# Pooling's buffers moved into the upper half of Y, late loads of the heads, and one PSUM bank for a head's two value products

## The chip, the cores and the metric

The kernel runs on one core of a Trainium2 chip. The metric is the device time of one execution in microseconds (us), the median of several runs.

## What is computed

A two-layer decoder trunk on x of 512 positions by 2048 channels, fp32. The change lies in the even layer, whose mixer is:

```
z = h @ w_in                                   # 2048 x 12288
a_in, a_gate, q, k, v, b_gate = split(z)       # a: 1024 wide, q/k/v: 3 groups x 8 heads x 128
ya = causal_pool_mixer(a_in, pool_w, pool_scale) * silu(a_gate)
yb = dilated_attention(q, k, v, cos, sin) * silu(b_gate)
return concatenate([ya, yb]) @ w_out
```

The pooling mixer takes causal means over windows of 2, 4, 8 and 16 positions for four groups of channels, subtracts the input and multiplies by a 256x256 matrix for each group. The attention has 8 heads; each head adds three patterns: group 0 is a window of 128 positions in natural order, groups 1 and 2 take positions of one residue modulo 4 together, so their queries stand in a permuted order (residue r first, then i, for position 4i + r). One softmax denominator serves all three.

## The kernel before

Every fp32 weight is split into a high part (`whi`, ScalarE, line 69) and a rest (`wlo`, VectorE, line 70), and each product is three TensorE matmuls. SyncE loads weights in 512 KB chunks into 4 raw buffers (`wraw`, line 111). A split chunk is a part, and 4 parts can stand ready. The program is a list of stages, one part each (`run_section`). Most of the input projection goes by `pair_item`: two 128-channel units u and v computed with shared half products, in stages s0 to s7. Stage s0 (lines 300 to 304) makes 24 narrow products (256 columns) in a bank and ScalarE copies half of it to u's buffer (line 294); s1 makes 12 more and is copied too; s3 and s3b make 24, s5 and s7 another 24, and s4 and s6 together 24 wide ones (512 columns). Stage s2 of a pair, which ends u, is put behind s1 of the next pair.

The first section is the attention's. Its q and k rows of the three groups of a head take turns in 8 slots, Y[:, 8] to Y[:, 15]; the last head (7) has slots 2 to 7, and slots 0 and 1 hold group 2 of head 6. V of groups 0 and 2 stands in Y[:, 0:8]. A head's attention (lines 665 to 742) is a generator that is advanced a step after each stage, so that a head's softmax runs beside the next head's projection: scores (lines 680 and 692), mask, maximum over keys (line 709, GpSimd), exponentials (lines 716 and 719, ScalarE), sum over keys (line 709 again), the value products (lines 725 to 732), then the reciprocal of the denominator, two multiplications (lines 738 to 740) and a store by GpSimd's queue to DRAM (`ybd`, line 741). The value products of group 0 go to bank `oa`, those of groups 1 and 2 to bank `ob` in permuted order; line 735 copies oa to SBUF, and line 736 adds ob to it with the order undone by a stride of 4.

After the section, lines 1053 to 1055 run out what is left of the last head and release its pool `att`. The pool `mixp`, opened at line 1057, takes the same memory, and the first access to a tile of a new pool waits for the release of the pool that was there, that is, for the store of the last head too. In `mixp` stand the four row buffers `xp` of the pooling (and of its gates), the split results `ph` and `pl` and others. The running sums `pa`, `pb` and `t` stand in Y[:, 4:8]. Lines 1066 and 1067 load the eight stored heads into Y[:, 8:16] on SyncE's queue as slots come free.

The pooling section runs four pairs for the rows (`a_after` makes sums, means and the split), two items of small products (`mix_item`), three pairs and two single items for the gates. `split_y(range(8, 16))` (lines 565 and 566) reads the loaded heads in the middle of the last single item. A scheduler orders each engine's instructions by readiness in a model of the time and by place in the program; `later` pins an instruction behind what was traced before it on its engine. Engines issue in order.

Of the kernel before, what the change touches and what calls it, by code (L numbers as in the profile page):

```python
# [13 lines left out]
F32 = mybir.dt.float32  # L14
FR = mybir.dt.float32r
AF = mybir.ActivationFunctionType
OP = mybir.AluOpType
AX = mybir.AxisListType

P = 128  # L20
D = 2048
S = 512
# [116 lines left out]
def trunk(ctx: ExitStack, tc: tile.TileContext, x, xt, out, ewv, ewz, ewo, epw, epost,  # L139
          owv, owz, owo, opost, osg, osb, oswt, osbias, cblob, rope, pcol):  # L140
    nc = tc.nc
# [27 lines left out]
    def sbank(name):  # L169
        return pss.tile([P, S], F32, tag="s", name=name)  # L170
# [450 lines left out]
    def vtile(g, t):  # L621
        return V1[:, t, :] if g == 1 else Y[:, 2 * g + t, :]
# [6 lines left out]
    def perm_in(ap):  # L629
        return ap.rearrange("p (i r) -> p r i", r=4)  # L630

    def perm_out(ap):
        return ap.rearrange("p (r i) -> p r i", r=4)
# [31 lines left out]
    def attention(h, qk, gates):  # L665
        vc = slice((h % 4) * P, (h % 4) * P + P)
        sa = att.tile([P, 4, 256], F32, tag="sa", name=f"sa{h}")
        sg = att.tile([P, 2, S], F32, tag="sg", name=f"sg{h}")

        def temp(name):  # L670
            return att.tile([P, S], F32, tag="tmp", name=f"{name}{h}", bufs=3)

        own, prev = sa[:, :, 0:P], sa[:, 0:3, P:]
        q, k = qk["q0"], qk["k0"]
        mA = cb[:, C_MA:C_MA + 256]
        b0 = sbank(f"sa{h}").rearrange("p (n k) -> p n k", n=2)
        b1 = sbank(f"sb{h}").rearrange("p (n k) -> p n k", n=2)
        for m in range(4):
            b, w_ = (b0, b1)[m // 2][:, m % 2, :], 256 if m < 3 else P
            nc.tensor.matmul(b[:, 0:w_], k[:, P * m:P * m + P], q[:, P * m:P * m + w_], start=True, stop=True)  # L680
        nc.vector.scalar_tensor_tensor(sa[:, 0:2, :], b0, SCALE, mA[:, None, :].to_broadcast([P, 2, 256]),
                                       op0=OP.mult, op1=OP.min)
        sal = sa.rearrange("p n k -> p (n k)")
        for m in (2, 3):
            w_ = 256 if m < 3 else P
            nc.vector.scalar_tensor_tensor(sa[:, m, 0:w_], b1[:, m - 2, 0:w_], SCALE, mA[:, 0:w_],
                                           op0=OP.mult, op1=OP.min)
        for g in (1, 2):
            b = sbank(f"sg{h}_{g}")
            for r in range(4):  # L690
                t = slice(P * r, P * r + P)
                nc.tensor.matmul(b[:, t], qk[f"k{g}"][:, t], qk[f"q{g}"][:, t], start=True, stop=True)
            mB = cb[:, C_MB + P * (g - 1):C_MB + P * g]
            nc.vector.scalar_tensor_tensor(sg[:, g - 1, :].rearrange("p (r i) -> p r i", r=4),
                                           b.rearrange("p (r i) -> p r i", r=4), SCALE,
                                           mB[:, None, :].to_broadcast([P, 4, P]), op0=OP.mult, op1=OP.min)

        def natural(t):
            return t.rearrange("p (r i) -> p i r", r=4)

        def reduced(op, rop, name):
            u, v = temp(f"{name}u"), temp(f"{name}v")
            nc.vector.tensor_tensor(u, sg[:, 0, :], sg[:, 1, :], op=op)
            nc.vector.tensor_tensor(v.rearrange("p (i r) -> p i r", r=4), natural(u),
                                    sa[:, :, 0:P].rearrange("p n (i r) -> p n i r", r=4), op=op)
            v3 = v[:, P:].rearrange("p (n k) -> p n k", n=3)
            nc.vector.tensor_tensor(v3, v3, prev, op=op)
            w_ = temp(f"{name}w")
            nc.gpsimd.partition_all_reduce(w_, v, P, rop)
            return w_  # L710

        m = reduced(OP.max, bass_isa.ReduceOp.max, "m")
        yield 4
        nc.vector.tensor_tensor(own, own, m.rearrange("p (n k) -> p n k", n=4), op=OP.subtract)
        nc.vector.tensor_tensor(prev, prev, m[:, P:].rearrange("p (n k) -> p n k", n=3), op=OP.subtract)
        nc.scalar.activation(sal[:, 0:896], sal[:, 0:896], AF.Exp)
        for g in range(2):
            nc.vector.tensor_tensor(perm_out(sg[:, g, :]), perm_out(sg[:, g, :]), perm_in(m), op=OP.subtract)
        nc.scalar.activation(sg, sg, AF.Exp)
        den = reduced(OP.add, bass_isa.ReduceOp.add, "d")  # L720
        yield 2
        oa = sbank(f"oa{h}")
        for n in range(4):
            o = oa[:, P * n:P * n + P]
            nc.tensor.matmul(o, vtile(0, n)[:, vc], sa[:, n, 0:P], start=True, stop=n == 0)
            if n:
                nc.tensor.matmul(o, vtile(0, n - 1)[:, vc], sa[:, n - 1, P:], start=False, stop=True)
        ob = sbank(f"ob{h}")
        for r in range(4):
            t = slice(P * r, P * r + P)  # L730
            nc.tensor.matmul(ob[:, t], vtile(1, r)[:, vc], sg[:, 0, t], start=True, stop=False)
            nc.tensor.matmul(ob[:, t], vtile(2, r)[:, vc], sg[:, 1, t], start=False, stop=True)
        y = gates[h]
        oas = temp("o")
        nc.scalar.activation(oas, oa, AF.Copy)
        nc.vector.tensor_tensor(perm_in(oas), perm_out(ob), perm_in(oas), op=OP.add)
        yield 2
        nc.vector.reciprocal(den, den)
        nc.vector.tensor_tensor(y, y, den, op=OP.mult)
        nc.vector.tensor_tensor(y, y, oas, op=OP.mult)  # L740
        nc.gpsimd.dma_start(ybd[h], y)
        yield 1

# [39 lines left out]
    mix = {}  # L783
# [19 lines left out]

    def mix_dst(j, key):
        def dst():
            t = mix["xp"][mix["n"] % 4]
            mix["n"] += 1
            mix[f"{key}{j}"] = t
            return t[:, 16:272], t[:, 272:]
        return dst  # L810

    def a_after(j):
        def after():
            g = j // 2
            w_ = WINDOWS[g]
            xp, pa, pb = mix[f"a{j}"], mix["pa"], mix["pb"]
            src, sh = xp, 1
            while sh < w_:
                dst = pb if src is pa else pa
                nc.vector.tensor_tensor(dst[:, 16:], src[:, 16:], src[:, 16 - sh:16 - sh + S], op=OP.add)  # L820
                src, sh = dst, 2 * sh
            t = mix["t"]
            nc.vector.scalar_tensor_tensor(t, src[:, 16:], 1.0 / w_, xp[:, 16:], op0=OP.mult, op1=OP.subtract)
            ic = cb[:, C_IC + 16 * g:C_IC + 16 * g + 16]
            nc.vector.tensor_tensor(src[:, 16:32], src[:, 16:32], ic, op=OP.mult)
            nc.vector.tensor_tensor(t[:, 0:16], src[:, 16:32], xp[:, 16:32], op=OP.subtract)
            ph = mix["pool"].tile([P, S], FR, tag="ph", name=f"ph{j}", bufs=6)
            pl = mix["pool"].tile([P, S], FR, tag="pl", name=f"pl{j}", bufs=6)
            nc.scalar.activation(ph, t, AF.Copy)
            nc.vector.tensor_tensor(pl, t, ph.bitcast(F32), op=OP.subtract)  # L830
            pooled[j] = (ph, pl)
        return after

    def agate_mult(j, t):
# [1 line left out]

    def agate_after(j):
        def after():
            t = mix[f"g{j}"][:, 16:]
            nc.scalar.activation(t, t, AF.Silu)  # L840
            agate_mult(j, t)
        return after

    def agate_direct(j):
        def after(ps):
            t = mix_dst(j, "g")() and mix[f"g{j}"][:, 16:]
            nc.scalar.activation(t, ps, AF.Silu)
            agate_mult(j, t)
            if j == 7:
                split_y(range(0, 8))  # L850
        return after
# [205 lines left out]
    with tc.tile_pool(name="mixp", bufs=1) as mp:  # L1057
        mix["pool"] = mp
        post["junk"] = mp.tile([P, S], mybir.dt.bfloat16, name="junk0")
        work = Y[:, 4:8, :].rearrange("p a b -> p (a b)")  # L1060
        mix["pa"], mix["pb"], mix["t"] = work[:, 0:528], work[:, 528:1056], work[:, 1056:1568]
        mix["xp"] = [mp.tile([P, 16 + S], F32, name=f"xp{i}") for i in range(4)]
        mix["n"] = 0
        for t in mix["xp"] + [mix["pa"], mix["pb"]]:
            nc.gpsimd.memset(t[:, 0:16], 0.0)
        for h in range(8):
            nc.sync.dma_start(Y[:, 8 + h, :], ybd[h])
        run_section(1)
        post["g"] = rrow(2, "gpost0")
        later(nc.sync.dma_start(post["g"], epost.partition_broadcast(P)))  # L1070
        run_section(2)
# [112 lines left out]
```

## Time and profile before

| what | us |
|---|---|
| median of 3 runs (2047.17 to 2047.47) | 2047.44 |
| the profiled execution | 2048.37 |
| its span, first to last instruction | 2046.6 |
| TensorE busy in the span | 2010.9 |
| VectorE busy | 1426.9 |
| ScalarE busy | 786.7 |

Busy times are those of one profiled execution. Matmuls are pipelined, so the start-to-start distance of two rows is the time that a matmul takes, and the duration in its row is longer.

### The profile page before, as it was taken

How to read it: one execution, taken by the hardware profiler on the slowest of the kernel's cores; microseconds unless marked ns; L12 is line 12 of the kernel's file. 1: busy time of each engine (PE TensorE's matmuls, PEld its weight loads, DVE VectorE, ACT ScalarE, POOL GpSimd, SP SyncE). 2: the span in 40 equal slices, each digit the busy share in tenths (PEclk: the TensorE clock that was granted, in tenths of full speed). 3: DMA queues.
4: the chain of work that ended last, by engine and by line, in shares of the span. 5: the costliest groups of instructions: out<-in, count | busy, mean ns of one | idle time of the engine just before them, and what ended most of it. 6: DMA issues, size and time to landing. Idle time of an engine off the chain costs nothing.

```text
span 2046.6 us, 26314 instructions
## 1 busy us (share of the span) xinstructions
PE 2010.9 (98%) x10576; PEld 1747.6 (85%) x10576; DVE 1426.9 (70%) x1887; ACT 786.7 (38%) x1089; POOL 99.9 (5%) x97
## 2 busy tenths in 40 slices
PE   8999999999999999995999999999999999999998
PEld 8988989899989999985888888888888889988886
DVE  5748889885228889886764435775899998854255
ACT  6433434432224434432443324653222224533243
POOL 1000001101000001101000000210000001000002
PEclk9999999999999999997999999999999999999999
DMA  8322332333222332331333336865233323243465
GB/s 322 93 82 83 93 111 86 94 108 99 92 83 84 92 117 84 98 119 47 112 104 114 113 98 223 292 209 158 80 96 100 91 75 104 83 134 113 134 213 178
DMA packets 70284, 246.23 MB, mean 120 GB/s; under 512 B 8049, under 2 KB 8305, under 8 KB 68881
## 3 DMA queue, kind: packets, MB, share of 16 engines
q1 hardware_dynamic: 68304, 236.15, 36.6%
q0 software_dynamic: 1856, 8.39, 1.1%
q8 instruction: 83, 1.36, 0.3%
q14 instruction: 41, 0.33, 0.1%
HBM read 234.02 MB, written 10.49 MB: 119 GB/s over the span
## 4 chain that ended last, share of the span: by engine, by line
PE 97%; DVE 1%; issue 0%; POOL 0%; DMA 0%; ACT 0%; SPq 0%; DVEq 0%; POOLq 0%; ACTq 0%
PE n L371 12%; PE n L373 12%; PE n L372 12%; PE z L251 5%; PE z L249 5%; PE z L250 5%; PE a L276 5%; PE a L278 5%; PE a L277 5%; PE b L285 4%; PE b L287 4%; PE b L286 4%; PE a L285 4%; PE a L286 4%; PE a L287 4%; PE b L277 2%
## 5 line engine op out<-in xcount | busy, mean ns | idle before, releaser
L70 DVE TENSOR_TENSOR wlo<-wraw,whi 128x1024 fp32r<-128x1024 f32 (+1 forms) x529 | 577.8, 1099 | 423.6 <-ACT whi L69 419.9
L69 ACT ACTIVATE whi<-wraw 128x1024 fp32r<-128x1024 f32 (+1 forms) x529 | 499.1, 955 | 842.0 <-PE n L373 350.7
L371 PE MATMUL n<-whi,Al 128*128 128x512 f32 x1024 | 405.0, 398 | 6.4 <-DVE Al L481 6.4
L372 PE MATMUL n<-wlo,Ah 128*128 128x512 f32 x1024 | 407.0, 397 | 0.0
L373 PE MATMUL n<-whi,Ah 128*128 128x512 f32 x1024 | 406.1, 397 | 0.0
L371 PEld LDWEIGHTS n<-whi,Al 128*128 128x128 f32 x1024 | 223.4, 218 | 41.8 <-DVE Al L481 6.4
L372 PEld LDWEIGHTS n<-wlo,Ah 128*128 128x128 f32 x1024 | 223.4, 218 | 35.4
L373 PEld LDWEIGHTS n<-whi,Ah 128*128 128x128 f32 x1024 | 223.3, 218 | 35.4
L249 PE MATMUL z<-Ah,wlo 128*128 128x512 f32 x448 | 177.9, 397 | 0.0
L250 PE MATMUL z<-Al,whi 128*128 128x512 f32 x448 | 177.2, 396 | 0.0
L251 PE MATMUL z<-Ah,whi 128*128 128x512 f32 x448 | 177.2, 395 | 0.0
L939 DVE SCALAR_TENSOR_TENSOR Y<-dp,pc,Y 128x512 f32<-128x512 f32 x240 | 168.6, 745 | 0.9
L277 PE MATMUL a<-Al,whi 128*128 128x256 f32 x504 | 141.3, 281 | 0.0
L276 PE MATMUL a<-Ah,wlo 128*128 128x256 f32 x504 | 141.3, 282 | 0.0
L278 PE MATMUL a<-Ah,whi 128*128 128x256 f32 x504 | 141.0, 282 | 0.0
L285 PE MATMUL a<-Ah,wlo 128*128 128x512 f32 x336 | 133.6, 398 | 0.0
L285 PE MATMUL b<-Ah,wlo 128*128 128x512 f32 x336 | 133.2, 396 | 0.0
L286 PE MATMUL a<-Al,whi 128*128 128x512 f32 x336 | 132.9, 395 | 0.0
L287 PE MATMUL a<-Ah,whi 128*128 128x512 f32 x336 | 132.8, 395 | 0.0
L286 PE MATMUL b<-Al,whi 128*128 128x512 f32 x336 | 132.7, 395 | 0.0
L287 PE MATMUL b<-Ah,whi 128*128 128x512 f32 x336 | 132.6, 395 | 0.0
L276 PE MATMUL a<-S,wlo 128*128 128x256 f32 x336 | 95.8, 285 | 10.2 <-ACT xp L294 10.2
(210 smaller groups left out, 3163.1 us busy)
## 6 DMA issues: line engine op xcount, KB each, us to landing
wraw<-in_ewz_dram SPq DMA_DIRECT2D x144, 512.0 KB, 3.8
wraw<-in_owz_dram SPq DMA_DIRECT2D x80, 512.0 KB, 3.7
wraw<-in_ewo_dram SPq DMA_DIRECT2D x48, 512.0 KB, 4.2
wraw<-in_owo_dram SPq DMA_DIRECT2D x48, 512.0 KB, 3.7
wraw<-in_ewv_dram SPq DMA_DIRECT2D x47, 512.0 KB, 3.6
wraw<-in_owv_dram SPq DMA_DIRECT2D x32, 512.0 KB, 3.7
xn<-in_x_dram SPq DMA_DIRECT2D x4, 1024.0 KB, 12.1
xr<-in_x_dram SPq DMA_DIRECT2D x16, 256.0 KB, 5.8
```

Source lines behind the costliest of these rows:

```text
L69: self.nc.scalar.activation(hi, raw, AF.Copy)
L70: self.nc.vector.tensor_tensor(lo, raw, hi.bitcast(F32), op=OP.subtract)
L249: nc.tensor.matmul(ps, wl[:, j], Ah[:, k, :], start=first, stop=False)
L250: nc.tensor.matmul(ps, wh[:, j], Al[:, k, :], start=False, stop=False)
L276: nc.tensor.matmul(out, wl[:, j], fh[:, j, :], start=start and j == 0, stop=False, skip_group_check=True)
L277: nc.tensor.matmul(out, wh[:, j], fl[:, j, :], start=False, stop=False, skip_group_check=True)
L285: nc.tensor.matmul(out, wl[:, k], Ah[:, k, :], start=False, stop=False, skip_group_check=True)
L286: nc.tensor.matmul(out, wh[:, k], Al[:, k, :], start=False, stop=False, skip_group_check=True)
L287: nc.tensor.matmul(out, wh[:, k], Ah[:, k, :], start=False, stop=k == ks[-1], skip_group_check=True)
L371: nc.tensor.matmul(ps, tok(Al, k, t), wh[:, j], start=first, stop=False)
L372: nc.tensor.matmul(ps, tok(Ah, k, t), wl[:, j], start=False, stop=False)
L373: state["mm"] = nc.tensor.matmul(ps, tok(Ah, k, t), wh[:, j], start=False, stop=last).ins
```

## The change

The row buffers `xp`, `pa`, `pb` and `t` become pieces of Y[:, 8:16]; the gates get tiles of their own (`gt`) in `mixp`; the loads of the heads are traced after the sums of row 6, behind all earlier work of SyncE's queue. In the attention, both value products of a head add into one bank `o`, where groups 1 and 2 write with a stride of 4 elements (`oi`), the copy and the addition are gone, and line 740's multiplication reads the bank.

```diff
-        oa = sbank(f"oa{h}")
+        o = sbank(f"o{h}")
+        oi = perm_in(o)
         for n in range(4):
-            o = oa[:, P * n:P * n + P]
-            nc.tensor.matmul(o, vtile(0, n)[:, vc], sa[:, n, 0:P], start=True, stop=n == 0)
+            nc.tensor.matmul(o[:, P * n:P * n + P], vtile(0, n)[:, vc], sa[:, n, 0:P], start=n == 0, stop=False,
+                             skip_group_check=True)
             if n:
-                nc.tensor.matmul(o, vtile(0, n - 1)[:, vc], sa[:, n - 1, P:], start=False, stop=True)
-        ob = sbank(f"ob{h}")
+                nc.tensor.matmul(o[:, P * n:P * n + P], vtile(0, n - 1)[:, vc], sa[:, n - 1, P:], start=False, stop=False,
+                                 skip_group_check=True)
         for r in range(4):
             t = slice(P * r, P * r + P)
-            nc.tensor.matmul(ob[:, t], vtile(1, r)[:, vc], sg[:, 0, t], start=True, stop=False)
-            nc.tensor.matmul(ob[:, t], vtile(2, r)[:, vc], sg[:, 1, t], start=False, stop=True)
+            nc.tensor.matmul(oi[:, r, :], vtile(1, r)[:, vc], sg[:, 0, t], start=False, stop=False, skip_group_check=True)
+            nc.tensor.matmul(oi[:, r, :], vtile(2, r)[:, vc], sg[:, 1, t], start=False, stop=r == 3, skip_group_check=True)
         y = gates[h]
-        oas = temp("o")
-        nc.scalar.activation(oas, oa, AF.Copy)
-        nc.vector.tensor_tensor(perm_in(oas), perm_out(ob), perm_in(oas), op=OP.add)
...
-        nc.vector.tensor_tensor(y, y, oas, op=OP.mult)
+        nc.vector.tensor_tensor(y, y, o, op=OP.mult)
...
-            t = mix["xp"][mix["n"] % 4]
-            mix["n"] += 1
+            t = mix["xp"][j % 4] if key == "a" else mix["pool"].tile([P, S], F32, tag="gt", name=f"gt{j}", bufs=4)
...
+            if j == 6:
+                for h in range(8):
+                    later(nc.sync.dma_start(Y[:, 8 + h, :], ybd[h]))
...
-            t = mix_dst(j, "g")() and mix[f"g{j}"][:, 16:]
+            t = mix["pool"].tile([P, S], F32, tag="gt", name=f"gt{j}", bufs=4)
...
-        work = Y[:, 4:8, :].rearrange("p a b -> p (a b)")
-        mix["pa"], mix["pb"], mix["t"] = work[:, 0:528], work[:, 528:1056], work[:, 1056:1568]
-        mix["xp"] = [mp.tile([P, 16 + S], F32, name=f"xp{i}") for i in range(4)]
-        mix["n"] = 0
+        work = Y[:, 8:16, :].rearrange("p a b -> p (a b)")
+        mix["xp"] = [work[:, 528 * i:528 * i + 528] for i in range(4)]
+        mix["pa"], mix["pb"], mix["t"] = work[:, 2112:2640], work[:, 2640:3168], work[:, 3168:3680]
         for t in mix["xp"] + [mix["pa"], mix["pb"]]:
             nc.gpsimd.memset(t[:, 0:16], 0.0)
-        for h in range(8):
-            nc.sync.dma_start(Y[:, 8 + h, :], ybd[h])
         run_section(1)
```

## Rows read from the trace of the kernel before

**Rows 1.** The page's first part: busy us, share of the span, instructions.

```profile
PE 2010.9 (98%) x10576; PEld 1747.6 (85%) x10576; DVE 1426.9 (70%) x1887; ACT 786.7 (38%) x1089; POOL 99.9 (5%) x97
```

**Rows 2.** Waits of TensorE over the span: us in total, times, longest.

```profile
PE a L276 <- ACT xp L294: 10.2, 1, 10.2
PE oa L725 <- ACT sa L716: 7.3, 1, 7.3
...
PE sg L692 <- DVE Y L662: 3.3, 1, 3.3
```

**Rows 3.** Stretches: us, busy us of each engine, granted clock, DMA share, GB/s.

```profile
155.00:915.00 760.00, 760.00 (x4552) 690.98 (x4552) 590.54 (x798) 295.97 (x407) 45.54 (x23) 1.00 0.31 96
...
932.00:943.00 11.00, 3.70 (x17) 3.41 (x17) 7.32 (x10) 2.01 (x2) 1.77 (x1) 0.50 0.09 25
943.00:957.00 14.00, 3.84 (x24) 3.65 (x23) 6.90 (x6) 1.25 (x3) 4.09 (x6) 0.62 0.10 36
```

**Rows 4.** TensorE's timeline where the sections meet: start, duration, [idle before <- releaser].

```profile
925.45 0.28 PE L276 MATMUL b<-S,wlo 128*128 128x256 f32 x1
...
926.77 0.28 PE L278 MATMUL b<-S,whi 128*128 128x256 f32 x1
930.35 2.05 PE L692 MATMUL sg<-Y 128*128 128x128 f32 x8 [3.30 <-DVE Y L662]
939.69 1.22 PE L725 MATMUL oa<-sa,Y 128*128 128x128 f32 x4 [7.30 <-ACT sa L716]
...
955.50 0.58 PE L276 MATMUL a<-S,wlo 128*128 128x256 f32 x1 [10.16 <-ACT xp L294]
...
960.79 0.52 PE L285 MATMUL b<-Ah,wlo 128*128 128x512 f32 x1
```

**Rows 5.** Head 6: the chain's scores (16 records), then TensorE's timeline around the value products.

```profile
844.68 1.79 PE sg L692 x16
...
873.17 0.60 PE L725 MATMUL oa<-sa,Y 128*128 128x128 f32 x4
...
876.43 0.36 PE L276 MATMUL b<-S,wlo 128*128 128x256 f32 x1
...
877.34 0.39 PE L285 MATMUL a<-Ah,wlo 128*128 128x512 f32 x1
...
878.04 0.39 PE L285 MATMUL a<-Ah,wlo 128*128 128x512 f32 x1
```

**Rows 6.** ScalarE's timeline: the first copy of the pooling.

```profile
955.07 0.38 ACT L294 ACTIVATE xp<-a 128x256 f32<-128x256 f32 x1 [10.82 <-DMA ybd<-y]
```

**Rows 7.** VectorE's timeline: end of the last rotation, end of the last head.

```profile
929.52 0.68 DVE L662 TENSOR_TENSOR Y<-Y,sw 32x512 f32<-32x512 f32 x1
...
951.68 0.69 DVE L740 TENSOR_TENSOR y<-y,o 128x512 f32<-128x512 f32 x1
```

**Rows 8.** Groups by line: the removed copy and addition (busy us, mean ns | idle before).

```profile
L735 ACT ACTIVATE o<-oa 128x512 f32<-128x512 f32 x8 | 4.7, 589 | 4.4 <-PE oa L727 2.5 <-DVE dv L704 1.9
...
L736 DVE TENSOR_TENSOR o<-ob,o 128x512 f32<-128x512 f32 x8 | 8.6, 1080 | 2.4 <-PE ob L732 2.4
L740 DVE TENSOR_TENSOR y<-y,o 128x512 f32<-128x512 f32 x8 | 5.4, 678 | 0.1
```

**Rows 9.** Weight loads of line 371: strided by 4 (75 to 100 us), plain (120 to 145 us).

```profile
L371 PEld LDWEIGHTS n<-whi,Al 128*128 128x128 f32 x36 | 11.1, 307 | 0.0
...
L371 PEld LDWEIGHTS n<-whi,Al 128*128 128x128 f32 x35 | 6.6, 187 | 1.6
```

**Rows 10.** Line 731: records, duration ns min/median/max, first and last start.

```profile
L731 PE MATMUL ob<-sg,V x64: 275/275/421, 254.2 to 944.8; 128*128 128x128 f32 x64
```

**Rows 11.** The heads' loads (median us to landing), the end of row 6's sums, the first split_y.

```profile
Y<-ybd SPq DMA_DIRECT2D x8, 256.0 KB, 2.7
...
1058.03 0.68 DVE L830 TENSOR_TENSOR pl<-Y,ph 128x512 fp32r<-128x512 f32 x1
...
L565 ACT ACTIVATE Ah<-Y x16: 615/622/636, 1125.8 to 1138.0; 128x512 fp32r<-128x512 f32 x16
```

More of the change, by code (lines that the diff above doesn't have):

```diff
@@ L805, in dst @@
         def dst():
-            t = mix["xp"][mix["n"] % 4]
-            mix["n"] += 1
+            t = mix["xp"][j % 4] if key == "a" else mix["pool"].tile([P, S], F32, tag="gt", name=f"gt{j}", bufs=4)
             mix[f"{key}{j}"] = t
-            return t[:, 16:272], t[:, 272:]
+            t = t[:, 16:] if key == "a" else t
+            return t[:, 0:256], t[:, 256:]
         return dst
@@ L838, in after @@
         def after():
-            t = mix[f"g{j}"][:, 16:]
+            t = mix[f"g{j}"]
             nc.scalar.activation(t, t, AF.Silu)
```

## The prediction

> **What bounds the kernel now.** I read the page first: TensorE is busy 2010.9 of 2046.6 us [rows 1], so no other engine's work is worth anything by itself, and what can be won is TensorE's idle time of some 36 us. The waits of TensorE say where it is: 20.8 us lie in three waits [rows 2], the rest is the start and the end of the kernel, which the change does not touch. All three waits stand in one place, the meeting of the attention's and the pooling's section. The stretches show how special that place is: from 155 to 915 us, with seven heads' softmax running beside the projections, TensorE has not one idle microsecond at a granted clock of 1.00; from 932 to 957 us it is busy 7.5 of 25 us at 0.50 to 0.62 [rows 3], that is, partly on the lower of the clock's two levels, 1.2 GHz.
>
> TensorE's timeline tells why [rows 4]. It ends the pooling's s1 (last start at 926.77), waits for the rotated q of the last head, makes its scores, waits for the exponentials, makes the value products, and then waits 10.16 us for ScalarE's first copy into `xp`. That copy came at 955.07 because the last head's store had to land [rows 6]: `xp` lies in memory that the attention's pool gives back only then. So from 927 us on there is nothing in TensorE's queue but the last head, and the whole chain of that head, from the end of the rotation at 930.2 (929.52 + 0.68) to the last multiplication at 952.4 [rows 7], lies open, where the chains of the earlier heads run beside projections.
>
> **The change, part by part.**
>
> *Row buffers in Y.* Rows 0 and 1 of the pooling are written to slots 8 to 10 of Y (each buffer has 528 columns, a slot 512). Their last readers are the scores of head 6 (at 844.68 [rows 5]) and, for 32 columns, the group 0 scores of head 7, which TensorE has made stages before the section's end. So the copies of s0 and s1 need nothing of the last head any more, and TensorE can go on with the products of s3, s3b and so on, with the last head's matmuls between them. What is the stretch worth? From the end of s1 (926.77 plus one step of 0.12, 926.89) to the start of s4 at 960.79 TensorE takes 33.9 us. The work in it is: 8 records of scores, which at full clock take 0.89 (half of the 1.79 for 16 of head 6); the value products, 876.43 - 873.17 = 3.26 at full clock [rows 5]; 24 narrow products at 0.12 (the 11 steps from 925.45 to 926.77 [rows 4]), 2.88. Sum 7.03. So the most that can be won is 33.9 - 7.0 = **26.9 us**: the three waits (20.8) and some 6 us of work at the lower clock.
>
> *What stays.* The wait for the rotated q, 3.30 us [rows 2, 4], is VectorE's backlog of rotations and splits, and the change does not shorten it. If the scheduler puts s3 and s3b (2.88 us) ahead of the scores, it is filled; if it leaves the scores in front, it stays, and the row behind it shows what else it costs: the scores took 2.05 instead of 0.89 us, the clock was already down, so up to 3 us more go until it is back. Bounds: 0 and 6.3 us. I take 3.3, the wait itself, as in the row, about midway.
>
> *The rest of the last head.* Its chain costs VectorE 14.2 us (7.32 + 6.90 [rows 3]) in some 22, and beside it now come the pooling's splits. In the seven heads before, VectorE was busy 590.54 of 760 us [rows 3] and TensorE never waited, and four parts can stand ready. I cost this at nothing; what hides it are those prepared parts, and without them each microsecond by which VectorE is late would be one of TensorE's. The sums of the first two rows need `ph`, a tile of `mixp`, and so still wait for the last store; nobody reads them before the small products two pairs later.
>
> *Copy and addition removed.* 8 times 589 ns of ScalarE and 8 times 1080 ns of VectorE [rows 8], both beside a TensorE that is always busy for seven heads: nothing on the path. For the last head the addition lay beside GpSimd's sum, nothing either. Line 740 now reads the bank instead of SBUF; for its 678 ns [rows 8] the same cover holds. The bank stays occupied until then, two stages longer; the next head asks for it a head later.
>
> *Strided writes to the bank.* 64 matmuls (8 heads by 8; line 731 shows 64 records, two for each matmul, and line 732 as many [rows 10]) now write with a step of 4 elements. No row of before shows TensorE writing so. At full clock the 15 value products of a head take 3.26 us, 0.217 each [rows 5], so the 64 take 13.9 us, and each is on the path, since TensorE is. The nearest rows of other accesses with this step: VectorE 1080 ns against 678 [rows 8], a weight load 307 ns against 187 [rows 9], both 1.6 times. By that, 8.3 us would be lost; the other end is 0. But the weight load is of operands read, not of results written, and an fp32 matmul puts out a column much more slowly than the kernel's other matmuls: 0.217 us for 128 columns, where a wide product takes 0.233 us ((878.04 - 877.34) / 3) for 512 [rows 5]. The bank keeps up with four columns in that time when they stand side by side, so I take 0 and keep 8.3, and a doubling of 13.9, for the range.
>
> Against this stands a rule of the Trainium skill, "PSUM — Partial Sum Buffer", section Specifications (TRN2): lines of 8 bytes, and any access pattern that isn't contiguous slows matmuls significantly. By it the sum would be worse by some such amount as in the rivals below; no run here shows it yet.
>
> *Late loads.* Eight issues on SyncE's queue move from the meeting of the sections to behind the sums of row 6, which ended at 1058.03; each lands 2.7 us after issue, and the first reader comes at 1125.8 [rows 11]. All times here move forward together, so about 68 us are there for some 22 (8 by 2.7, one after the other). Nothing, unless the queue stands at the first of them with weight loads behind it; four raw buffers and four parts cover some microseconds.
>
> *Running sums and pads.* `pa`, `pb` and `t` become free with the last scores instead of the last value products: earlier than their first use. The six pad settings stay. Nothing.
>
> **Sum:** 26.9 - 3.3 = 23.6 us gained. The profiled execution took 2048.37, 0.93 above the median of 2047.44; from the former 2024.8, from the median **2023.8**. Its own range is 26.9 + 0.5 to 26.9 - 6.3 - 1.5 won, 2020 to 2028.
>
> **Rivals.**
>
> *A: strided writes cost double.* +13.9 us: 2037.7. For: both rows of other engines at 1.6. Against: the slow rate of columns of an fp32 matmul.
>
> *B: slower through the same strided writes.* It decides from a factor of 1 + 23.6 / 13.9 = 2.7 on. At 4 the 64 matmuls cost 41.7 us: 2023.8 + 41.7 = 2065.5. For: an accumulating write must read, add and write, and each element would be alone in its line. Against: no row with that step exceeds 1.7 times.
>
> *C: the last head still stands in front, elsewhere.* ScalarE's first `ph`, or a pad setting on GpSimd behind the last store, is issued in order while the store is out; the splits behind it come late. TensorE would have the prepared parts of the first pair: 2.88 us (s3, s3b), 24 narrow (2.88) and 24 wide products at 0.233 (5.6), scores and value products (4.15): 15.5 us, until 942.4. If the store lands as in before at 955 and the next split takes 2 us, 14.6 us of wait remain, and some 3 at the lower clock: 26.9 - 17.6 = 9.3 won, 2038.1. For: the engines issue in order. Against: readiness decides the order, and these instructions are known to be late.
>
> *D: the wait moves to a copy that is just as late.* If row 1's buffer waited for all of slot 10's head, or the value products were put ahead of everything, TensorE's order would be as before: 2047, no change. Against: the readers named above are done.
>
> **How the numbers follow.** Main case 0.62, A 0.17, C 0.10, B and its like 0.06, D 0.05. The main case, A and C win, 0.89 together, of which a point goes to a C that ends behind the start: faster 0.88, same 0.05 (D), slower 0.07 (B and that point). Within 0.2% (4.1 us) a measurement of this kernel can't be told from no change. The range from 2019.5 to 2039 holds the main case, A and C.
>
> **What would show it.** Right: TensorE has no wait for `xp` any more and the granted clock between 930 and 960 us is near 1.00; the copies of line 294 into Y follow each other before the last head's store; lines 731 and 732 start 0.11 us apart as before. If the latter start farther apart by 0.1 us or more, A or B is it. If TensorE waits in that stretch for `whi` or `wlo`, with ScalarE or VectorE held by `ph` or a pad, C. A wait for Y's heads before 1125 or a SyncE queue that stands at the late loads while TensorE starves would be a price that I left at nothing. The forecast is wrong if the span falls by less than 15 us with the strided matmuls at their old pace.

## The result, and the profile after

The changed kernel takes 2021.05 us (median of 4 runs, 2020.69 to 2022.04) against 2047.31 of the kernel before in the same comparison: 26.3 us less, ratio 0.9873, 95% interval 0.9856 to 0.9891. The profiled execution took 2020.69 us, its span is 2018.9.

The page's first part, and TensorE's waits over the whole span:

```profile
PE 2003.8 (99%) x10576; PEld 1742.6 (86%) x10576; DVE 1421.5 (70%) x1879; ACT 783.5 (39%) x1081; POOL 98.1 (5%) x97
```

```profile
PE n L371 <- DVE Al L481: 6.5, 1, 6.5
```

One wait is left, in the kernel's first section; the three of [rows 2] are gone. TensorE's busy time fell as well, from 2010.9 to 2003.8 us, though it ran the same 10576 instructions. That part is the clock, as the stretches show (the same as in [rows 3]: us, busy us by engine, granted clock, DMA share, GB/s):

```profile
155.00:915.00 760.00, 760.00 (x4552) 691.26 (x4552) 585.55 (x791) 293.31 (x400) 43.81 (x27) 1.00 0.30 95
...
932.00:943.00 11.00, 11.00 (x81) 10.36 (x80) 10.64 (x16) 5.34 (x9) 1.78 (x1) 1.00 0.12 41
943.00:957.00 14.00, 14.00 (x89) 12.50 (x88) 13.52 (x15) 5.69 (x7) 3.53 (x1) 1.00 0.39 119
```

Where TensorE was busy 7.5 of 25 us at 0.50 to 0.62, it is busy 25 of 25 at 1.00. VectorE is busy 24.2 of the 25 with the last head, the splits and the pooling's sums, and TensorE waits for none of it.

TensorE's timeline at the same place, to be laid beside [rows 4]:

```profile
925.70 0.28 PE L278 MATMUL b<-S,whi 128*128 128x256 f32 x1
925.82 0.28 PE L276 MATMUL a<-S,wlo 128*128 128x256 f32 x1
...
928.58 0.28 PE L278 MATMUL b<-S,whi 128*128 128x256 f32 x1
...
931.49 0.28 PE L276 MATMUL a<-S,wlo 128*128 128x256 f32 x1
931.61 0.28 PE L277 MATMUL a<-S,whi 128*128 128x256 f32 x1
931.73 1.06 PE L692 MATMUL sg<-Y 128*128 128x128 f32 x8
932.54 0.36 PE L278 MATMUL a<-S,whi 128*128 128x256 f32 x1
...
948.86 0.61 PE L725 MATMUL o<-sa,Y 128*128 128x128 f32 x4
...
951.99 0.39 PE L733 MATMUL o<-sg,Y 128*128 128x128 f32 x2
```

Right behind s1's last matmul come s3 and s3b (925.82 to 928.58), then the wide products of s4 and the first of s6 (the gap in these lines), and only inside s5 the scores at 931.73. The rotated q was ready by then: VectorE's timeline, with the end of the rotation and of the last head as in [rows 7],

```profile
928.57 0.67 DVE L662 TENSOR_TENSOR Y<-Y,sw 32x512 f32<-32x512 f32 x1
...
953.87 3.35 DVE L736 RECIPROCAL dw<-dw 128x512 f32<-128x512 f32 x1 [0.48 <-POOL dw L709]
...
959.42 0.68 DVE L738 TENSOR_TENSOR y<-y,o 128x512 f32<-128x512 f32 x1
```

shows it ending at 929.24. The last head now ends at 960.1 instead of 952.4: it is slower, and it costs nothing, because work lies beside it. On ScalarE the pooling's copies go into Y from 924 us on, and the first tile of the new pool waits for the store:

```profile
924.17 0.86 ACT L294 ACTIVATE Y<-a 128x256 f32<-128x256 f32 x2 [0.88 <-DVE Y L297]
...
963.25 0.63 ACT L827 ACTIVATE ph<-Y 128x512 fp32r<-128x512 f32 x1 [0.80 <-DMA ybd<-y]
```

(A row of x2 may hold a copy of the attention's last unit as well as the pooling's first.) The same wait that cost 10.82 us in [rows 6] is 0.80 us here, and it is `ph`'s, which nobody needs soon.

### The profile page after: what moved, and what is told of

It is laid out like the page before. It is cut to its first block, busy times and chain, and to the rows that moved or that the text cites. A ratio compares the mean times of both kernels' runs of the same rounds, so it can differ in the third digit from the quotient of the medians.

```text
span 2018.9 us, 26291 instructions
## 1 busy us (share of the span) xinstructions
PE 2003.8 (99%) x10576; PEld 1742.6 (86%) x10576; DVE 1421.5 (70%) x1879; ACT 783.5 (39%) x1081; POOL 98.1 (5%) x97
## 4 chain that ended last, share of the span: by engine, by line
PE 99%; DVE 0%; DMA 0%; POOL 0%; ACT 0%; SPq 0%; issue 0%; DVEq 0%; POOLq 0%; ACTq 0%
PE n L371 12%; PE n L372 12%; PE n L373 12%; PE z L250 5%; PE z L251 5%; PE z L249 5%; PE a L278 5%; PE a L277 5%; PE a L276 5%; PE b L285 4%; PE a L285 4%; PE a L287 4%; PE a L286 4%; PE b L287 4%; PE b L286 4%; PE b L277 2%
## 5 line engine op out<-in xcount | busy, mean ns | idle before, releaser
L294 ACT ACTIVATE Y<-a 128x256 f32<-128x256 f32 x112 | 58.4, 529 | 148.9 <-PE a L278 143.7
```

## The experiments

**Which part of the change brings the time?** Two kernels, each with one half. First the changed kernel with two banks, copy and addition put back:

```diff
-        o = sbank(f"o{h}")
-        oi = perm_in(o)
+        oa = sbank(f"oa{h}")
...
+        ob = sbank(f"ob{h}")
...
+        nc.scalar.activation(oas, oa, AF.Copy)
+        nc.vector.tensor_tensor(perm_in(oas), perm_out(ob), perm_in(oas), op=OP.add)
```

> The changed kernel with the attention's two banks, copy and addition put back; buffers in Y, gate tiles and late loads stay. Theory (the gain is the row buffers' alone, and the steps of 4 in the bank cost nothing): 2021 us, within 2 us of the changed kernel, ratio to before 0.987. Rival (the one bank brings part of the gain, by a shorter chain of the last head or less work on VectorE): 2 to 10 us more than the changed kernel. Rival (the strided writes cost time that the gain hides): below 2019 us.

Measured: 2021.16 us, ratio 0.9869 (0.9854 to 0.9884). The first half (row buffers in Y, with the gate tiles and late loads that go with them) gives the whole gain. Then the kernel before with the one bank alone (the same lines, the other way round):

> The kernel before with only the one bank: both value products in it, no copy, no addition. Theory: 2047 us, no change within 0.2%, the wait for the row buffer's copy still about 10 us, since the copy and the addition lay beside GpSimd's sum. Rival (they lay on the last head's open chain): some 1.7 us less (0.6 + 1.1), 2045.6. Rival (strided writes cost double): 2061.

Measured: 2047.69 us against 2047.73, ratio 1.0000 (0.9991 to 1.0009). TensorE's waits in it:

```profile
PE a L276 <- ACT xp L294: 10.7, 1, 10.7
PE o L725 <- ACT sa L716: 7.2, 1, 7.2
...
PE sg L692 <- DVE Y L662: 3.3, 1, 3.3
```

are those of [rows 2], with a new one of 0.5 us for a split. So the one bank is worth nothing that can be seen in either kernel: the interval reaches 0.09%, or 1.8 us, to either side, where a doubling of the strided products would be 13.9 us. That the writes are not paid for by the copy and the addition that went is shown by the products' own pace, in the last experiment.

**Is it the release of the whole pool?** The kernel before, with the pooling's pool waiting tile by tile:

```diff
-    with tc.tile_pool(name="mixp", bufs=1) as mp:
+    with tc.tile_pool(name="mixp", bufs=1, reuse_waits="tile") as mp:
```

> The kernel before, except that a tile of the pooling's pool waits only for the tiles of the attention's pool that stood in its own bytes, not for the release of all of them. Theory (what delays the section is the release of the whole pool, with the last head's store): the third wait of 10.2 us goes or shrinks, 2037 to 2041 us, and if the row buffers lie on tiles that are free before the last head's chain, all three go, 2021 to 2026. Rival (the bytes themselves are in use until the end, by the gate row or the temporaries): 2047.

Measured: 2035.08 us, ratio 0.9938 (0.9924 to 0.9951). ScalarE's first copy, and TensorE's waits:

```profile
944.12 0.38 ACT L294 ACTIVATE xp<-a 128x256 f32<-128x256 f32 x1 [0.49 <-PE ob L731]
```

```profile
PE oa L725 <- ACT sa L716: 7.3, 1, 7.3
...
PE sg L692 <- DVE Y L662: 3.3, 1, 3.3
PE a L276 <- ACT xp L294: 0.2, 1, 0.2
```

The copy comes at 944.12 instead of 955.07 and now waits for the last value products of line 731. These read `V1`, the V of group 1, a tile of the attention's pool, so the row buffer evidently stands on its bytes. The third wait is down to 0.2 us, and the gain of 12.6 us is that wait and some of the lower clock behind it: from 943 to 957 us the granted clock is 1.00, where it was 0.62 ([rows 3]). The 2037 of the expectation is the wait alone. The other two waits stay, because the copy is still behind the value products and TensorE has nothing else. So the release (with the store) was the cause of the third wait only; the first two needed row buffers that are free before the head's chain, which is what the move to Y gives.

**Why did the wait for the rotated q not stay?** The changed kernel, with s3's products of the first pooling pair held behind the last head's scores:

```diff
+                with tc.issue_after(mix["scores"]):
+                    product("a", XL, hi[:, Rt], lo[:, Rt], "S2")
```

> The changed kernel with the products of the first pooling pair's s3 issued only behind the last head's scores on TensorE, so that nothing can fill the wait for the rotated q. Theory (that wait of 3.3 us was left in the forecast's sum and is filled by s3 and s3b in the changed kernel): the wait comes back, with or without a stretch at the lower clock, 3 to 6.5 us more than the changed kernel, 2024 to 2027.5 us. Rival (other work of the pair fills it, or the queue of VectorE is shorter now): 2021.

Measured: 2022.26 us, ratio 0.9874 (0.9857 to 0.9890), the same as the changed kernel's. TensorE's timeline:

```profile
928.08 0.38 PE L276 MATMUL b<-S,wlo 128*128 128x256 f32 x1 [0.47 <-ACT Y L294]
...
929.61 0.40 PE L285 MATMUL b<-Ah,wlo 128*128 128x512 f32 x1
...
934.04 1.05 PE L696 MATMUL sg<-Y 128*128 128x128 f32 x8
```

and VectorE's end of the rotation:

```profile
930.17 0.67 DVE L666 TENSOR_TENSOR Y<-Y,sw 32x512 f32<-32x512 f32 x1
```

The rival was right: with s3 taken away, s3b (from 928.08) and the wide products of s4 and s6 (from 929.61), which go to the other bank, fill the time until the rotated q is ready at 930.84 and beyond, at the price of one wait of 0.47 us. (The edit holds s3's products alone; to hold these too was not tried.)

**What would the wait for the store cost if it stood in front?** The forecast's case C, brought about by an edit: four splits on ScalarE are issued only behind the first `ph`.

```diff
+            with self.tc.issue_after(self.behind):
+                self.nc.scalar.activation(hi, raw, AF.Copy)
```

> The changed kernel with four splits of weights on ScalarE issued only behind the first ph, the first tile of the pooling's pool, which waits for the last head's store. It is the forecast's case C made on purpose. Theory (only the order on ScalarE keeps this wait off TensorE): TensorE waits for the high parts, 8 to 18 us more than the changed kernel, 2029 to 2039 us, with a stretch at the lower clock. Rival (the prepared parts cover it): 2021 to 2024.

Measured: 2039.47 us, ratio 0.9958 (0.9943 to 0.9973): some 18 us of the 26 are lost, just above the upper end of what was expected. ScalarE's timeline, then TensorE's wait (lines are shifted by the edit):

```profile
960.17 0.63 ACT L833 ACTIVATE ph<-Y 128x512 fp32r<-128x512 f32 x1 [13.88 <-DMA ybd<-y]
960.70 3.46 ACT L73 ACTIVATE whi<-wraw 128x1024 fp32r<-128x1024 f32 x4
```

```profile
PE a L291 <- DVE wlo L76: 14.1, 1, 14.1
```

and the stretch behind it:

```profile
957.00:972.00 15.00, 8.94 (x29) 7.15 (x30) 5.08 (x7) 4.28 (x6) 0.56 (x1) 0.59 0.47 157
```

ScalarE stands 13.88 us at `ph`, and TensorE 14.1 us at the split behind it, from 949.0 to 963.1 us. The rest is two shorter waits (0.6 and 0.5 us) and the lower clock: 0.59 from 957 to 972 us. The new pool's wait is still there in the changed kernel, and it is only the order on ScalarE that keeps it off TensorE.

**Are the late loads free, and how late may they be?** The changed kernel with the loads traced directly ahead of their reader:

```diff
             if ci == 0:
+                for h in range(8):
+                    later(nc.sync.dma_start(Y[:, 8 + h, :], ybd[h]))
                 split_y(range(8, 16))
```

> The changed kernel with the eight loads of the heads put directly ahead of their first reader, in the middle of the last gate item, behind all earlier work of SyncE's queue. Theory (the late loads of the changed kernel are free because some 70 us lie between them and their reader, and are not free without that): TensorE waits for the high parts of the loaded heads between the end of the section and the output projection, 3 to 12 us, 2024 to 2033 us. Rival (the order of readers gives enough time even so): 2021.

Measured: 2021.42 us, ratio 0.9872 (0.9859 to 0.9885). The theory's second half was wrong. SyncE's timeline, then ScalarE's:

```profile
1100.50 4.59 SPq L866 DMA_DIRECT2D Y<-ybd  x8
```

```profile
1103.80 0.62 ACT L565 ACTIVATE Ah<-Y 128x512 fp32r<-128x512 f32 x1
1104.80 6.37 ACT L565 ACTIVATE Ah<-Y 128x512 fp32r<-128x512 f32 x12 [0.39 <-DMA Y<-ybd]
```

Eight issues take 4.6 us, the first row is read 3.3 us after its issue, and ScalarE takes 0.5 to 0.6 us for each row: it waits 0.39 us once and TensorE not at all. In the changed kernel itself the loads go out earlier than that, on SyncE from 1005.65 to 1031.66 us:

```profile
1005.65 0.81 SPq L832 DMA_DIRECT2D Y<-ybd  x2
...
1027.02 4.63 SPq L832 DMA_DIRECT2D Y<-ybd  x6
```

The first reader comes at 1097.9. So the slack is some 66 us, and all of it could be given away.

**Does TensorE pay for strided writes at all?** The changed kernel with 96 bf16 matmuls of 512 columns added, which nobody reads: 32 plain, 32 with a step of 2 elements in the bank, 32 with a step of 4.

```diff
+                for n in range(32):
+                    nc.tensor.matmul(by4.rearrange("p (i r) -> p r i", r=4), bf[:, 0:P], bf, start=n == 0, stop=n == 31)
```

> The changed kernel with 96 extra bf16 matmuls of 512 columns in the middle of the last gate item, whose results nobody reads: 32 write their bank side by side, 32 with a step of 2 elements, 32 with a step of 4. Theory (the fp32 value products escape a cost of strided writes because they put out columns at a quarter of the rate of a wide matmul): the plain ones start 0.21 to 0.24 us apart, those with steps 1.5 to 2.2 times that, 0.33 to 0.5. Rival (strided writes cost TensorE nothing at any rate): all three the same. The extra work makes the kernel 21 us longer if nothing costs, 36 to 55 us if the steps do.

Measured: one run, 2055.08 us, its span 34.4 us longer than the changed kernel's, just below the 36 to 55 that were expected if the steps cost. TensorE's timeline (plain, step 2, step 4; the other 11 plain ones stand further ahead), then the stretches of the two groups with a step:

```profile
1104.35 4.71 PE L873 MATMUL plain<-junk 128*128 128x512 bf16 x21
1108.90 13.90 PE L875 MATMUL by<-junk 128*128 128x512 bf16 x32
1122.59 13.94 PE L877 MATMUL by<-junk 128*128 128x512 bf16 x32
```

```profile
1109.00:1122.00 13.00, 13.00 (x32) 4.17 (x30) 0.00 (x0) 0.00 (x0) 0.00 (x0) 1.00 0.09 35
1122.50:1135.00 12.50, 12.50 (x30) 4.03 (x29) 0.00 (x0) 0.00 (x0) 0.00 (x0) 1.00 0.00 0
```

From start to start: 21 plain ones take 4.55 us, 0.217 each; 32 with step 2 take 13.69, 0.428 each; step 4 the same. A step of either size halves the rate of these matmuls, to 0.428 / 512 = 0.84 ns a column. It is not the lower clock, at which 512 columns look much the same (0.43 us from start to start at a clock of 0.50, from 963.1 to 968.7 us in the run of case C): the granted clock is 1.00 in both stretches. The value products of the changed kernel are not slowed, as head 6 shows:

```profile
872.10 0.61 PE L725 MATMUL o<-sa,Y 128*128 128x128 f32 x4
872.54 0.39 PE L728 MATMUL o<-sa,Y 128*128 128x128 f32 x2
...
873.66 0.39 PE L732 MATMUL o<-sg,V 128*128 128x128 f32 x2
873.88 0.39 PE L733 MATMUL o<-sg,Y 128*128 128x128 f32 x2
...
875.00 0.39 PE L732 MATMUL o<-sg,V 128*128 128x128 f32 x2
875.22 0.39 PE L733 MATMUL o<-sg,Y 128*128 128x128 f32 x2
```

From 873.66 to 875.22 there are seven steps of 0.223 us; the plain products of the same head just before, from 872.54 to 873.66, make five of 0.224. Each matmul has two records, so a record takes 0.111 us for 128 columns, 0.87 ns a column. If each record writes its columns once, that is just slower than the 0.84 of the strided bf16 matmuls, which would explain why nothing is lost; but the traces don't show how often a record writes, and the bf16 matmuls differ in type and width as well as in pace, so this reason is not shown.

## Why the prediction was right, point by point

*What bounds the kernel.* Right: the time went out of the place and the three waits that [rows 2] name, and out of the lower clock beside them; seven heads' stretch is unchanged.

*Row buffers.* The ceiling of 26.9 us was right. The spans differ by 27.7 us and the medians by 26.3, on either side of it, and with runs of one kernel 1.4 us apart the two can't be told from it. Of the 27.7, 1.1 us lie ahead of the place: the value products of head 6 start at 872.10 here and at 873.17 before ([rows 5]). That offset goes with the run (873.21 with two banks put back, 872.27 in the run of case C), and without it 26.6 are left. The first half of the change does it alone (two banks put back: 2021.16).

*What stays.* This is the term that was mis-sized: "I take 3.3, the wait itself"; it measured 0. The time itself was there as forecast: the rotated q was ready at 929.24, 3.4 us behind the end of s1 at 925.82. But it was filled, as in the bound of 0 that the forecast gave, by s3 and s3b in front of the scores, with wide products behind them. The run with s3 held back says that it didn't hang on s3: other products of the same pair fill a wait of this length almost as well. With 0 in its place the sum is 2047.44 - 26.9 = 2020.5.

*The rest of the last head.* Right that it costs nothing, though VectorE was busy 24.2 of 25 us and the head ended 7.7 us later. The 0.8 us left are no measure of the room: with two banks put back VectorE was busy for all of 943 to 957 us, and TensorE still didn't wait.

*Copy, addition, one bank.* Right: nothing that the two runs can tell, in either direction.

*Strided writes.* Right at 0. The reason given, that an fp32 matmul puts out its columns slowly, fits but is not shown. By the forecast's count, one write a column in 0.223 us, a column has 1.74 ns, twice the 0.84 of a strided bf16 matmul; by the records it has 0.87, a near thing, and then the choice of 0 had some luck in it. The comparison with VectorE and the weight load (1.6 times) was no guide. The rule of the Trainium skill, "PSUM — Partial Sum Buffer", section Specifications (TRN2), agrees with the bf16 runs (1.97 times for either step) and not with the fp32 matmuls of this kernel, which it does not set apart. Case A's doubling is what the bf16 matmuls show; case B's factor of 2.7 and more is seen in no run.

*Late loads.* Right at 0. The forecast's slack of 68 us is 66 in the trace.

*Case C.* It did not happen, but it is real: brought about by an edit it gave 2039.5, where the forecast worked out 2038.1 and a wait of 14.6 us (14.1 measured). That the two waits are so close is partly luck: TensorE ran dry at 949.0 and not at 942.4, and the split came at 963.1 and not at 957, both some 6 us late. Case D did not happen; the first copies go out at 924 us.

## What to carry to other kernels

Where two sections of a kernel meet, look first at what the first write of the new section waits for: memory of a pool that is released as a whole ties the section's start to the last store of the one before, and the engine that bounds the kernel then sees every chain that was hidden until there. Give the first buffers of the new section memory whose last reader is long done, and let the tiles that must wait be those that are needed late. An operation that was taken away, or a load that was put later, was worth nothing here beside a busy TensorE; price it by what lies beside it, not by its duration.

## What was not expected

A step of 2 in the bank costs a bf16 matmul as much as a step of 4 (0.428 us each, against 0.217), and the fp32 matmuls of this kernel pay nothing for a step of 4; a step of 2 was not tried on them. The wait of 3.3 us that nothing filled cost more than itself: the row of scores behind it took 2.05 us ([rows 4]), against 1.06 in the changed kernel (931.73 above), and the granted clock from 930.3 to 932.4 us was 0.51.
